# Eighteen feature tiles of a SwiGLU feed-forward by pairs, seven half products in place of eight

## The chip, the cores and the metric

The kernel runs on one core of a Trainium2 chip. The metric is device time in microseconds (us) of the whole kernel, taken over several runs; the trace is that of one execution. Five engines work side by side, each in the order of its own instructions: TensorE (PE, matrix products; PEld is its loading of stationaries), VectorE (DVE), ScalarE (ACT), GpSimd (POOL) and SyncE (SP, which here only issues transfers). Transfers between main memory and the on-chip memory (DMA) run beside them.

## What is computed

One layer of a hybrid decoder on 544 tokens (512 of a prompt, 32 of samples), in fp32. The part that the change touches is the feed-forward behind the second norm:

```python
    h2 = rmsnorm(x, norm2_g)
    x = x + (jax.nn.silu(h2 @ w_ffn_gate) * (h2 @ w_ffn_up)) @ w_ffn_down
```

The model width is 1024, the feed-forward width 2816: 22 feature tiles of 128 columns, each with a product for gate and one for up. Ahead of it lie an input projection, gated linear attention, dilated window attention, a merge and an output projection; behind it the down projection and a last norm.

## The kernel before

Features lie on the 128 partitions, tokens along the free axis, in two halves of 272 (`HA`). A product of 1024 inputs is 8 blocks `k` of 128. To reach fp32 accuracy each operand is split into a high and a low fp32r part (`split`: the high part on ACT, L229, the low part on DVE, L221 or, with a factor, L218), and each product is three: high by high, high by low, low by high. So one feature tile of gate is 8 blocks x 3 x 2 halves = 48 matmuls of 128x128 by 272 columns, all at L215.

Weights come as a stream of tiles in one order. `emit_w` takes the next: SP issues its transfer of 512 KB (`raw`, L260), ACT writes `wh` (and a sum into `mark`), DVE writes `wlo`, POOL copies one number of `mark` (`pace`, L280), which holds POOL back until then, and then issues one transfer of the window caches from memory to memory (L399). `raw`, `wh` and `wlo` have two buffers each, so a tile is prepared while another is multiplied.

In the feed-forward the loop `for m in range(2, NF)` does gate, then up, of one feature tile. `gated` takes the results out: ACT writes tanh into `ts`, DVE makes two operations on `ts` (the second with the product for up), then ACT and DVE split `ts` at once into `ah_m` and `al_m`, the operands of the down projection. That needs 22 blocks, in three weight tiles (`KB`) for each of 8 output tiles. The first two feature tiles are done by halves of the tokens, in between the second norm of the other half (`second`: for each of 8 blocks one operation on DVE, L218, and a split). `gfb`, the gains of the last norm spread over the partitions, is loaded through POOL's queue when a place in memory comes free (L411) and scaled by DVE (L1259), ahead of the first output tile.

The instructions of each engine are put in order by a scheduler ahead of time; an engine never steps past one that waits. Places in the on-chip memory are given by a table of slots at the head of the program.

Of the kernel before, what the change touches and what calls it, by code (L numbers as in the profile page):

```python
# [161 lines left out]
def build(tc, I, O, C):  # L162
# [89 lines left out]
    def emit_w(i, pin=lambda i: i, later=None):  # L252
        ap, k0, nk, c0, m, keep = wl[i]
        raw = wp.tile([P, 8, P], F32, tag="raw", name="raw", bufs=2)
# [906 lines left out]
    n2g = vec_tile("n2g", I["norm2_g"][0], 8)  # L1161
    h2h, h2l = [], []
    for i, (a_, b_) in enumerate(cols):
# [35 lines left out]
        def second(i=i, a_=a_, b_=b_, n=n, tiles=tiles, dgs=dgs):  # L1199
# [12 lines left out]
            if i:  # L1212
                free("acc", "sq", "rt", "r2i", "dg2", "h2")
# [154 lines left out]
```

## Time and profile before

| | |
|---|---|
| three runs | 1081.20, 1082.54 and 1085.53 us, median 1082.54 |
| profiled execution | span 1081.6 us from first to last instruction, no other time on record for it |
| PE busy | 1061.0 us, 98% |
| DVE, ACT, POOL busy | 52%, 38%, 28% |

"Busy" is time with an instruction under way. The profile gives each engine's own queue, what each idle stretch waited for, and the granted clock of TensorE (1.00 is 2.4 GHz, 0.50 is 1.2 GHz). The span lies 0.9 us under the median.

### The profile page before, as it was taken

How to read it: one execution, taken by the hardware profiler on the slowest of the kernel's cores; microseconds unless marked ns; L12 is line 12 of the kernel's file. 1: busy time of each engine (PE TensorE's matmuls, PEld its weight loads, DVE VectorE, ACT ScalarE, POOL GpSimd, SP SyncE). 2: the span in 40 equal slices, each digit the busy share in tenths (PEclk: the TensorE clock that was granted, in tenths of full speed). 3: DMA queues.
4: the chain of work that ended last, by engine and by line, in shares of the span. 5: the costliest groups of instructions: out<-in, count | busy, mean ns of one | idle time of the engine just before them, and what ended most of it. 6: DMA issues, size and time to landing. Idle time of an engine off the chain costs nothing.

```text
span 1081.6 us, 20287 instructions
## 1 busy us (share of the span) xinstructions
PE 1061.0 (98%) x8151; PEld 1025.4 (95%) x8151; DVE 559.7 (52%) x1061; ACT 413.4 (38%) x942; POOL 301.7 (28%) x485
## 2 busy tenths in 40 slices
PE   6999999999999999999999999999999999999997
PEld 5999898999999989989989999999999999999996
DVE  5687764685686645646544565533333333332332
ACT  5454445644464434433333343323232322222232
POOL 2533323233354312222212121122222222322221
PEclk8999999999999999999999999999999999999998
DMA  8588446665677626536424551245454545544442
GB/s 229 142 237 254 142 130 181 185 189 171 188 237 231 219 89 196 156 119 200 137 64 135 183 175 68 90 162 189 164 187 158 192 158 192 188 154 116 113 112 83
DMA packets 178286, 176.14 MB, mean 163 GB/s; under 512 B 9952, under 2 KB 163264, under 8 KB 176912
## 3 DMA queue, kind: packets, MB, share of 16 engines
q1 hardware_dynamic: 155632, 84.36, 28.1%
q0 software_dynamic: 16272, 86.19, 22.7%
q10 hardware_dynamic: 6288, 4.29, 1.3%
q8 instruction: 64, 1.05, 0.4%
q14 instruction: 30, 0.25, 0.1%
HBM read 162.99 MB, written 55.67 MB: 202 GB/s over the span
## 4 chain that ended last, share of the span: by engine, by line
PE 93%; DMA 3%; ACT 1%; DVE 1%; issue 0%; ACTq 0%; POOL 0%; POOLq 0%; DVEq 0%
PE d L215 72%; PE zo L215 5%; PE zB L215 3%; PE zs L215 2%; PE zw L215 2%; PE zl L215 2%; DMA raw<-in_w_in 1%; PE zf L215 1%; PE zu L215 1%; DMA raw<-in_w_out 1%; PE zA L215 1%; DMA x<-in_x_prompt 1%; PE zq L215 1%; PE zA L674 1%; PE zp L215 1%
## 5 line engine op out<-in xcount | busy, mean ns | idle before, releaser
L229 ACT ACTIVATE wh<-raw 128x1024 fp32r<-128x1024 f32 (+1 forms) x133 | 138.5, 1041 | 414.2 <-PE d L215 329.0
L280 POOL COPY pace<-mark 1x1 f32<-1x1 f32 x145 | 123.6, 853 | 590.1 <-ACT wh L229 538.1
L221 DVE TENSOR_TENSOR wlo<-raw,wh 128x1024 fp32r<-128x1024 f32 (+1 forms) x132 | 159.6, 1209 | 203.3 <-ACT wh L229 203.2
L215 PE MATMUL d<-h,wh 128*128 128x272 f32 x1344 | 226.4, 288 | 0.0
L215 PE MATMUL d<-hh,wh 128*128 128x272 f32 (+1 forms) x928 | 203.9, 297 | 3.3 <-ACT hh L229 2.2
L215 PE MATMUL d<-hl,wh 128*128 128x272 f32 (+1 forms) x928 | 201.8, 295 | 0.0
L215 PE MATMUL d<-hh,wlo 128*128 128x272 f32 x912 | 195.4, 293 | 0.0
L215 PEld LDWEIGHTS d<-h,wh 128*128 128x128 f32 x1344 | 191.4, 188 | 0.0
L215 PEld LDWEIGHTS d<-hh,wh 128*128 128x128 f32 (+1 forms) x928 | 148.6, 190 | 6.6 <-ACT hh L229 2.3
L215 PEld LDWEIGHTS d<-hl,wh 128*128 128x128 f32 (+1 forms) x928 | 148.2, 189 | 3.8 <-issue 2.7
L215 PEld LDWEIGHTS d<-hh,wlo 128*128 128x128 f32 x912 | 145.3, 190 | 0.6
L215 PE MATMUL d<-h,wlo 128*128 128x272 f32 x672 | 141.8, 288 | 0.0
L215 PEld LDWEIGHTS d<-h,wlo 128*128 128x128 f32 x672 | 106.6, 188 | 0.0
L215 PE MATMUL d<-ah,wh 128*128 128x272 f32 x308 | 64.2, 290 | 0.0
L215 PE MATMUL d<-ah,wlo 128*128 128x272 f32 x308 | 63.7, 288 | 0.0
L215 PE MATMUL d<-al,wh 128*128 128x272 f32 x308 | 63.5, 287 | 0.0
L221 DVE TENSOR_TENSOR qb<-kt,qb 128x512 f32<-128x512 f32 x48 | 33.0, 688 | 45.0 <-DMA qb<-qd_d 44.8
L215 PEld LDWEIGHTS d<-al,wh 128*128 128x128 f32 x308 | 48.3, 188 | 0.0
L215 PEld LDWEIGHTS d<-ah,wh 128*128 128x128 f32 x308 | 48.3, 188 | 0.1
L215 PEld LDWEIGHTS d<-ah,wlo 128*128 128x128 f32 x308 | 48.2, 188 | 0.0
L221 DVE TENSOR_TENSOR ts<-ts,d 128x544 f32<-128x544 f32 x21 | 15.1, 721 | 62.0 <-PE d L215 62.0
L411 POOL DMA_DIRECT2D kt<-in_state_win_k x48 | 32.9, 685 | 12.2 <-DVE qb L221 9.1
(438 smaller groups left out, 1756.2 us busy)
## 6 DMA issues: line engine op xcount, KB each, us to landing
raw<-in_w_in SPq DMA_DIRECT2D x58, 512.0 KB, 5.8
out_win_k_sample<-in_state_win_k POOLq DMA_DIRECT2D x32, 511.0 KB, 4.6
out_win_v_sample<-in_state_win_v POOLq DMA_DIRECT2D x32, 511.0 KB, 4.7
qb<-qd_d POOLq DMA_DIRECT2D x48, 256.0 KB, 5.1
raw<-in_w_ffn_gate SPq DMA_DIRECT2D x22, 512.0 KB, 5.6
raw<-in_w_ffn_up SPq DMA_DIRECT2D x22, 512.0 KB
kt<-in_state_win_k POOLq DMA_DIRECT2D x32, 256.0 KB, 5.3
vt<-in_state_win_v POOLq DMA_DIRECT2D x32, 256.0 KB, 4.2
```

The source lines that it names most:

```text
L215: return pe.matmul(out, lhsT=lhsT, rhs=rhs, start=start, stop=stop)
L221: return dve.tensor_tensor(out=out, in0=a, in1=b, op=op)
L229: pin(act.activation(out=hi, in_=src, func=AF.Copy, scale=scale, **kw))
L280: tc.keep_in_program_order(pool.tensor_copy(out=pace, in_=mark[0:1]))
L411: tc.keep_in_program_order((eng or nc.gpsimd).dma_start(out=t, in_=ap))
L674: pe.transpose(zA[:, v * P:(v + 1) * P], s[:, v * P:(v + 1) * P], ident)
```

## The change

Feature tiles 0 to 3 stay as they were (`PLAIN = 4`). The other 18 go by pairs, gate and up apart: 9 x 2 = 18 pair products. For one pair, weights (two feature tiles, split into two halves of the 8 blocks) and activations (two halves of the blocks, two halves of the tokens) are taken as 2x2 matrices of parts, and the four results come from seven products of parts, by Strassen's scheme, in place of eight. One such half product has 4 blocks x 3 = 12 matmuls of 272 columns, so a pair has 84.

What that needs:

- Sums of activations, formed once: `n5`, `n6`, `n4`, `n7`, each split in two parts; the normed activations (`hf`) are kept in fp32 until then, and `second` now does all eight operations on DVE ahead of the splits, two blocks at a time.
- Four sums of weights per pair, all on DVE (`sm` twice, `raw` twice, each 128x512), and the splits of five stationaries: `w12` and `w24` (1024 wide), `ws1`, `ws3`, `w22` (512 wide), each with one buffer for its high and one for its low part.
- The results are put together in `t4` by four operations on DVE; ACT copies the results of products 1 and 5 out first (`p1`, `p5`). The products go 1, 5, 2, 6, 7, 3, 4.
- The gated results stay in fp32 (`y_m`) and are split into `ah_m` and `al_m` for the down projection only when slots of the pair products come free, `ah_2` and `al_2` in the slots of `w22`, `gfb` in the slot of `w12h`.
- `raw`, `wh` and `wlo` share six buffers of one tag ("w"), in the whole kernel.

The core of the diff:

```diff
-    wp = opened(base, name="wp", bufs=3)
+    wp = opened(base, name="wp", bufs=6)
...
-        raw = wp.tile([P, 8, P], F32, tag="raw", name="raw", bufs=2)
+        raw = wp.tile([P, 8, P], F32, tag="w", name="raw")
...
-            for m in range(8):
-                t = two.tile([P, HA], F32, tag="h2", name="h2")
-                stt(t[:, 0:n], x2[m][:, a_:b_], n2g[:, m:m + 1], zb[:, 0:n], ALU.mult, ALU.mult)
-                split(h2h[i][m], h2l[i][m], t[:, 0:n])
...
+            for j in range(4):
+                for u in range(2):
+                    m = 2 * j + u
+                    stt(hf[i][j][:, u], x2[m][:, a_:b_], n2g[:, m:m + 1], zb[:, 0:n], ALU.mult, ALU.mult)
+                split(hi[j], lo[j], hf[i][j])
...
+    def prep_12(x):
+        mark = cst.tile([P, 1], F32, name="mark", bufs=8)
+        f = form("w12", raws[x][0], 8, accum_out=mark)
+        sta[x, 1], sta[x, 2] = halves_of(f, 0), halves_of(f, 1)
...
+    def prep_5(x):
+        (r1, r2), sm = raws[x], sms[x]
+        tt(sm[:, 0:4], r2[:, 0:4], r2[:, 4:8], ALU.add)
+        tt(sm[:, 4:8], r2[:, 0:4], r1[:, 0:4], ALU.add)
+        sta[x, 5] = form("ws1", sm[:, 0:4])
...
+    def prep_63(x):
+        r1 = raws[x][0]
+        tt(r1[:, 0:4], sms[x][:, 0:4], r1[:, 0:4], ALU.add)
+        tt(r1[:, 4:8], r1[:, 0:4], r1[:, 4:8], ALU.add)
+        f = form("w24", r1, 8)
+        sta[x, 6], sta[x, 3] = halves_of(f, 0), halves_of(f, 1)
...
+    def prep_7(x):
+        sta[x, 7] = form("ws3", sms[x][:, 4:8])
...
+    def prep_4(x):
+        sta[x, 4] = form("w22", raws[x][1][:, 4:8])
...
+    def product(x, n, z):
+        wh, wlo = sta.pop((x, n))
+        xh, xl = mov[n]
+        for k in range(4):
+            for j, (w, v) in enumerate(((wh, xh), (wh, xl), (wlo, xh))):
+                pin(mm(z, w[:, k], v(k), start=(k == 0 and j == 0), stop=(k == 3 and j == 2)))
...
+        product(x, 6, z[:, 1])
+        tt(t[:, 0:2], z, p1.to_broadcast([P, 2, HA]), ALU.add)
...
+        product(x, 7, z7)
+        tt(t[:, 2], z7, t[:, 1], ALU.add)
+        tt(t[:, 1:4:2], t[:, 1:3], p5.to_broadcast([P, 2, HA]), ALU.add)
...
+        product(x, 4, z[:, 1])
+        tt(t[:, 1:3], z, t[:, 1:3], ALU.add)
...
+    for m in range(NF):
+        ah.append(one.tile([P, NT], F32R, name=f"ah_{m}"))
+        al.append(one.tile([P, NT], F32R, name=f"al_{m}"))
+        split(ah[m], al[m], ym[m], 0.5)
+        free(f"y_{m}")
```

What it moves, at three places. SP's queue at the start of the program, before (a `raw` is a weight tile, an `xT_d` the store of one block of the transposed input):

```order
L260 DMA raw<-in_w_in 128x8x128 x2
L415 DMA xT_d<-xT_109 128x544
L415 DMA xT_d<-xT_110 128x544
L415 DMA xT_d<-xT_111 128x544
L415 DMA xT_d<-xT_112 128x544
L415 DMA xT_d<-xT_113 128x544
L415 DMA xT_d<-xT_114 128x544
L415 DMA xT_d<-xT_115 128x544
L415 DMA xT_d<-xT_116 128x544
L260 DMA raw<-in_w_in 128x8x128 x16
```

And now:

```order
L269 DMA raw<-in_w_in 128x8x128
L424 DMA xT_d<-xT_109 128x544
L424 DMA xT_d<-xT_110 128x544
L424 DMA xT_d<-xT_111 128x544
L424 DMA xT_d<-xT_112 128x544
L424 DMA xT_d<-xT_113 128x544
L424 DMA xT_d<-xT_114 128x544
L424 DMA xT_d<-xT_115 128x544
L424 DMA xT_d<-xT_116 128x544
L269 DMA raw<-in_w_in 128x8x128 x17
```

The second weight tile has moved behind the eight stores.

DVE's queue in the middle of the feed-forward, before: one feature tile is these five rows (numbers behind names tell buffers apart).

```order
L221 TENSOR_TENSOR wlo_9973<-raw_9969,wh_9972 128x1024
L218 SCALAR_TENSOR_TENSOR ts_10030<-ts_10030,d_9979 128x544
L221 TENSOR_TENSOR ts_10030<-ts_10030,d_10043 128x544
L221 TENSOR_TENSOR wlo_10037<-raw_10033,wh_10036 128x1024
L218 SCALAR_TENSOR_TENSOR al_15_10029<-ts_10030,ah_15_10028 128x544
```

And now, from the seventh product of one pair (`t4<-zs`) on: the rows at the turn to the next pair, twelve of fifteen.

```order
L230 TENSOR_TENSOR t4_9157<-zs_9229,t4_9157 128x272
L230 TENSOR_TENSOR raw_9018<-raw_9018 128x512
L230 TENSOR_TENSOR t4_9157<-t4_9157,p5_9186 128x2x272
L230 TENSOR_TENSOR w22l_9281<-raw_9019,w22h_9280 128x512
L230 TENSOR_TENSOR t4_9157<-d_9244,t4_9157 128x544
L230 TENSOR_TENSOR sm_9154<-raw_9153 128x512
L230 TENSOR_TENSOR sm_9154<-raw_9153,raw_9152 128x512
L230 TENSOR_TENSOR w24l_9260<-raw_9018,w24h_9259 128x1024
L227 SCALAR_TENSOR_TENSOR y_8_9284<-y_8_9284,t4_9157 128x544
L227 SCALAR_TENSOR_TENSOR y_9_9287<-y_9_9287,t4_9157 128x544
L230 TENSOR_TENSOR ws1l_9364<-sm_9154,ws1h_9363 128x512
L230 TENSOR_TENSOR w12l_9341<-raw_9152,w12h_9340 128x1024
```

Between the low part of `w22` and that of `w24`, both for the pair that PE takes next, now stand three other operations (`t4`, `sm`, `sm`).

DVE's queue at the turn to the down projection, before: the last split stands alone behind the last result, and `gfb` behind it.

```order
L221 TENSOR_TENSOR ts_10786<-ts_10786,d_10799 128x544
L221 TENSOR_TENSOR wlo_10793<-raw_10789,wh_10792 128x1024
L218 SCALAR_TENSOR_TENSOR al_21_10785<-ts_10786,ah_21_10784 128x544
L221 TENSOR_TENSOR wlo_10866<-raw_10862,wh_10865 128x768
L1259 TENSOR_SCALAR gfb_10851<-gfb_10851 128x1024
L1264 MEMSET ys_10859 128x45
```

And now (`t4_10927` belongs to the last pair; between the last two rows shown and `al_2` stand `al_10`, `al_9`, `al_16`, `al_15`, a `t4` of 544 columns, `al_12`, `al_11`, `al_14` and `al_13`):

```order
L230 TENSOR_TENSOR w24l_10887<-raw_10650,w24h_10886 128x1024
L230 TENSOR_TENSOR wlo_11130<-raw_11126,wh_11129 128x1024
L227 SCALAR_TENSOR_TENSOR al_6_11052<-y_6_9012,ah_6_11051 128x544
L227 SCALAR_TENSOR_TENSOR al_5_11048<-y_5_8743,ah_5_11047 128x544
L230 TENSOR_TENSOR t4_10927<-d_10958,p1_10941 128x544
L227 SCALAR_TENSOR_TENSOR y_20_10911<-y_20_10911,t4_10784 128x544
L227 SCALAR_TENSOR_TENSOR y_21_10914<-y_21_10914,t4_10784 128x544
L1440 TENSOR_SCALAR gfb_11115<-gfb_11115 128x1024
L1445 MEMSET ys_11123 128x45
L227 SCALAR_TENSOR_TENSOR al_19_11104<-y_19_10647,ah_19_11103 128x544
L227 SCALAR_TENSOR_TENSOR al_8_11060<-y_8_9284,ah_8_11059 128x544
L230 TENSOR_TENSOR t4_10927<-zs_10984,t4_10927 128x272
```

Sixteen of the low parts for the down projection have moved to this place, and `gfb` stands in the midst of them.

## Rows read from the trace of the kernel before

**Rows 1.** The page: span, and busy time of the engines.

```profile
span 1081.6 us, 20287 instructions
PE 1061.0 (98%) x8151; PEld 1025.4 (95%) x8151; DVE 559.7 (52%) x1061; ACT 413.4 (38%) x942; POOL 301.7 (28%) x485
```

**Rows 2.** Chain that ended last, pieces around the feed-forward: start us, us, what.

```profile
660.06 3.00 PE zw L215 x24
...
682.77 0.25 PE d L215 x2
...
694.82 264.20 PE d L215 x2100
```

**Rows 3.** Waits, 700 to 930 us: engine, line, releaser, us, times, longest.

```profile
DVE wlo L221 <- ACT wh L229: 86.2, 38, 4.6
DVE ts L221 <- PE d L215: 58.9, 19, 3.1
```

**Rows 4.** Timeline of SP, first and last of eight tiles of gate.

```profile
763.62 0.37 SPq L260 DMA_DIRECT2D raw<-in_w_ffn_gate  x1
...
848.18 0.37 SPq L260 DMA_DIRECT2D raw<-in_w_ffn_gate  x1
```

**Rows 5.** Instructions by form, 700 to 930 us: busy us, mean ns, idle before.

```profile
L221 DVE TENSOR_TENSOR wlo<-raw,wh 128x1024 fp32r<-128x1024 f32 x38 | 46.6, 1225 | 86.2 <-ACT wh L229 86.2
L221 DVE TENSOR_TENSOR ts<-ts,d 128x544 f32<-128x544 f32 x19 | 13.7, 721 | 58.9 <-PE d L215 58.9
```

**Rows 6.** The page, costliest groups: 128x512 on DVE.

```profile
L221 DVE TENSOR_TENSOR qb<-kt,qb 128x512 f32<-128x512 f32 x48 | 33.0, 688 | 45.0 <-DMA qb<-qd_d 44.8
```

**Rows 7.** Timeline of DVE: operations that follow each other without idle time.

```profile
693.48 0.71 DVE L218 SCALAR_TENSOR_TENSOR ts<-ts,d 128x544 f32<-128x544 f32 x1
694.11 1.22 DVE L221 TENSOR_TENSOR wlo<-raw,wh 128x1024 fp32r<-128x1024 f32 x1
695.25 0.71 DVE L221 TENSOR_TENSOR ts<-ts,d 128x544 f32<-128x544 f32 x1
695.88 0.43 DVE L218 SCALAR_TENSOR_TENSOR ts<-ts,zf 128x272 f32<-128x272 f32 x1
```

**Rows 8.** Timeline of DVE: an operation that reads what the one before wrote.

```profile
600.24 0.72 DVE L218 SCALAR_TENSOR_TENSOR ta<-ta,d 128x544 f32<-128x544 f32 x1 [2.71 <-PE d L215]
601.00 0.72 DVE L221 TENSOR_TENSOR ta<-ta,tb 128x544 f32<-128x544 f32 x1
```

**Rows 9.** Timelines of ACT and DVE: a split, and the operation behind it.

```profile
809.50 1.06 ACT L229 ACTIVATE wh<-raw 128x1024 fp32r<-128x1024 f32 x1 [4.42 <-PE d L215]
810.69 1.23 DVE L221 TENSOR_TENSOR wlo<-raw,wh 128x1024 fp32r<-128x1024 f32 x1 [4.26 <-ACT wh L229]
```

**Rows 10.** Timeline of SP at the start, and the page's transfer of a weight tile.

```profile
14.06 4.94 SPq L415 DMA_DIRECT2D xT_d<-xT  x8
raw<-in_w_in SPq DMA_DIRECT2D x58, 512.0 KB, 5.8
```

**Rows 11.** Timeline of DVE in the second norm.

```profile
679.62 0.90 DVE L218 SCALAR_TENSOR_TENSOR h<-xres,n2g,zb 128x272 f32<-128x272 f32 x2
```

**Rows 12.** Timeline where the down projection begins: PE, POOL, DVE.

```profile
936.26 0.42 PE L215 MATMUL d<-ah,wh 128*128 128x272 f32 x2
...
939.13 0.56 POOL L411 DMA_DIRECT2D gfb<-in_norm_f_g  x1
...
945.66 0.69 DVE L1259 TENSOR_SCALAR gfb<-gfb 128x1024 f32<-128x1024 f32 x1 [1.36 <-DMA gfb<-in_norm_f_g]
```

**Rows 13.** Timeline of PE around the start of the first product.

```profile
14.91 2.61 PE L215 MATMUL d<-dgt,ones 128*128 128x128 f32 x10 [1.68 <-DVE dgt L476]
...
19.73 0.82 PE L215 MATMUL d<-hh,wh 128*128 128x272 f32 x2 [2.21 <-ACT hh L229]
...
24.75 0.41 PE L215 MATMUL d<-hl,wh 128*128 128x272 f32 x2
```

**Rows 14.** Windows: span, busy of each engine, granted clock, DMA share, GB/s.

```profile
19.00:24.00 5.00, 4.11 (x15) 3.53 (x16) 4.97 (x7) 3.38 (x6) 0.17 (x1) 0.50 0.59 190
```

More of the change, by code (lines that the diff above doesn't have):

```diff
@@ L264, in emit_w @@
             step = 8
-            wh = [wp.tile([P, 8, P], F32R, tag="wh", name="wh", bufs=2)]
+            wh = [wp.tile([P, 8, P], F32R, tag="w", name="wh")]
             wlo = [wh[0][:, :, 2 * m:3 * m]]
@@ L380, in build @@
         W["wo", m] = want(I["w_out"][0], 0, 8, m * P, keep=f"wo{m}")
-    for m in range(NF):
+    for m in range(PLAIN):
         W["fg", m] = want(I["w_ffn_gate"][0], 0, 8, m * P, keep="fg1" if m == 1 else None)
@@ L1203, in second @@
                 (pin if i else nop)(mm(zb[:, c0:c1], ones[0:w_, :], dgt[0:w_, 0:w_]))
[L1204 to L1210 removed]
+            hi, lo = ([one.tile([P, 2, n], F32R, name=f"h2{i}{w}_{j}") for j in range(4)] for w in "hl")
+            hf.append([one.tile([P, 2, n], F32, name=f"hf{i}_{j}") for j in range(4)])
+            h2h.append([hi[k // 2][:, k % 2] for k in range(KD)])
+            h2l.append([lo[k // 2][:, k % 2] for k in range(KD)])
+            for j in range(4):
[3 more added lines that the diff above has]
+                split(hi[j], lo[j], hf[i][j])
             free(*[f"mg{i}_{m}" for m in range(8)])
             if i:
[L1213 removed]
+                free("acc", "sq", "rt", "r2i", "dg2")
         if i == 0:
@@ L1217, in build @@
             second()
-    ah, al = [], []
     F2, F2L = halved(h2h), halved(h2l)
+    ym = [None] * NF
     def gated(m, zg, zu, parts):
-        ah.append(one.tile([P, NT], F32R, name=f"ah_{m}"))
-        al.append(one.tile([P, NT], F32R, name=f"al_{m}"))
-        ts = two.tile([P, NT], F32, tag="ts", name="ts")
+        t = ym[m] = one.tile([P, NT], F32, name=f"y_{m}")
         for (a_, b_), g_, u_ in zip(parts, zg, zu):
-            t = ts[:, a_:b_]
-            act.activation(out=t, in_=g_, func=AF.Tanh, scale=0.5)
-            stt(t, t, 1.0, g_, ALU.add, ALU.mult)
-            tt(t, t, u_(), ALU.mult)
-            split(ah[m][:, a_:b_], al[m][:, a_:b_], t, 0.5)
+            act.activation(out=t[:, a_:b_], in_=g_, func=AF.Tanh, scale=0.5)
+            stt(t[:, a_:b_], t[:, a_:b_], 1.0, g_, ALU.add, ALU.mult)
+            tt(t[:, a_:b_], t[:, a_:b_], u_(), ALU.mult)
     z4 = {}
-    for hf in range(2):
+    for hf_ in range(2):
         for m in range(2):
@@ L1238, in build @@
                 if m == 0:
-                    z = z4.setdefault((nm, m), dense_ps() if hf == 0 else None)
+                    z = z4.setdefault((nm, m), dense_ps() if hf_ == 0 else None)
                 else:
                     z = z4.setdefault((nm, m), [None, None])
-                    z[hf] = mps("zf")[:, 0:cols[hf][1] - cols[hf][0]]
-                gemm(W[nm, m], F2, F2L, halves=(hf,), z=z, ahead=W["fu", 1] + hf * m - W[nm, m],
-                     fix=hf == 0, mid=(AT[m, nm], rates if m == 0 else second) if hf == 0 and (m, nm) in AT else None)
-            if hf == 1:
+                    z[hf_] = mps("zf")[:, 0:cols[hf_][1] - cols[hf_][0]]
+                gemm(W[nm, m], F2, F2L, halves=(hf_,), z=z, ahead=W["fu", 1] + hf_ * m - W[nm, m],
+                     fix=hf_ == 0, mid=(AT[m, nm], rates if m == 0 else second) if hf_ == 0 and (m, nm) in AT else None)
+            if hf_ == 1:
                 if m == 0:
@@ L1251, in build, with parts_of, operand @@
     dropped("fu1")
-    for m in range(2, NF):
-        zg = gemm(W["fg", m], F2, F2L)
-        gated(m, [zg], [lambda: gemm(W["fu", m], F2, F2L)], [(0, NT)])
-    free("ts", *[f"h2{i}_{m}" for i in range(2) for m in range(8)])
+    def parts_of(h, l):
+        return [lambda k, t=t: t[k // 2][:, k % 2] for t in (h, l)]
+    def operand(nm, src):
+        hi, lo = ([one.tile([P, 2, HA], F32R, name=f"{nm}{w}_{j}") for j in range(2)] for w in "hl")
+        for j in range(2):
+            split(hi[j], lo[j], src[j])
+        return parts_of(hi, lo)
@@ new lines, in by_halves, with summed_up @@
+    def by_halves(i, k0):
+        return [lambda k, t=t: t[i][k0 + k] for t in (h2h, h2l)]
+    B11, B12, B21, B22 = hf[0][0:2], hf[1][0:2], hf[0][2:4], hf[1][2:4]
+    mov = {1: by_halves(0, 0), 2: by_halves(0, 4), 3: by_halves(1, 4)}
+    def summed_up(nm, f):
+        ts_ = [two.tile([P, 2, HA], F32, tag="nf", name=nm, bufs=4) for _ in range(2)]
+        for j in range(2):
+            f(j, ts_[j])
+        return ts_
+    n5 = summed_up("n5", lambda j, t: tt(t, B11[j], B12[j], ALU.subtract))
@@ new lines, in build @@
+    mov[5] = operand("n5", n5)
+    n6 = summed_up("n6", lambda j, t: stt(t, n5[j], -1.0, B22[j], ALU.mult, ALU.subtract))
+    mov[6] = operand("n6", n6)
+    n4 = summed_up("n4", lambda j, t: stt(t, n6[j], -1.0, B21[j], ALU.mult, ALU.subtract))
+    mov[4] = operand("n4", n4)
+    n7 = summed_up("n7", lambda j, t: tt(t, B22[j], B12[j], ALU.subtract))
+    mov[7] = operand("n7", n7)
+    free("nf", *[f"hf{i}_{j}" for i in range(2) for j in range(4)])
+    pairs = [(nm, m) for m in range(PLAIN, NF, 2) for nm in ("fg", "fu")]
@@ new lines, in build, with fetch, form @@
+    src_of = {"fg": I["w_ffn_gate"][0], "fu": I["w_ffn_up"][0]}
+    raws, sms, sta = {}, {}, {}
+    def fetch(x):
+        nm, m = pairs[x]
+        r1, r2, sm = (wp.tile([P, 8, P], F32, tag="w", name=n) for n in ("raw", "raw", "sm"))
+        raws[x], sms[x] = (r1, r2), sm
+        c1, c2 = (src_of[nm][:, c * P:(c + 1) * P].rearrange("(k p) n -> p k n", p=P) for c in (m, m + 1))
+        nc.sync.dma_start(out=r1, in_=c1)
+        nc.sync.dma_start(out=r2, in_=c2)
+    def form(nm, src, n=4, **kw):
+        hi, lo = (two.tile([P, n, P], F32R, tag=f"{nm}{w}", name=f"{nm}{w}", bufs=1) for w in "hl")
+        split(hi, lo, src, **kw)
+        return hi, lo
@@ new lines, in halves_of @@
+    def halves_of(f, i):
+        return [t[:, 4 * i:4 * i + 4] for t in f]
+    def prep_12(x):
+        mark = cst.tile([P, 1], F32, name="mark", bufs=8)
+        f = form("w12", raws[x][0], 8, accum_out=mark)
+        sta[x, 1], sta[x, 2] = halves_of(f, 0), halves_of(f, 1)
+        pace = cst.tile([1, 1], F32, name="pace", bufs=2)
+        pin(pool.tensor_copy(out=pace, in_=mark[0:1]))
+        for _ in range(2):
+            if side_dma:
+                side_dma.pop(0)()
+    def prep_5(x):
[3 more added lines that the diff above has]
+        sta[x, 5] = form("ws1", sm[:, 0:4])
@@ new lines, in copied, with use @@
+    def copied(z, nm):
+        t = two.tile([P, 1, HA], F32, tag=nm, name=nm, bufs=1)
+        act.copy(out=t[:, 0], in_=z)
+        return t
+    def use(x, t):
+        nm, m = pairs[x]
+        for i in range(2):
+            g = t[:, 2 * i:2 * i + 2].rearrange("p a n -> p (a n)")
+            if nm == "fg":
+                y = ym[m + i] = one.tile([P, NT], F32, name=f"y_{m + i}")
+                act.activation(out=y, in_=g, func=AF.Tanh, scale=-0.5 if i else 0.5)
+                stt(y, y, 1.0, g, ALU.add, ALU.mult)
+            else:
+                tt(ym[m + i], ym[m + i], g, ALU.mult)
@@ new lines, in single, with double, pair @@
+    def single():
+        return mps("zs")[:, 0:HA]
+    def double():
+        z = psd.tile([P, 1024], F32, tag="d", name="d").rearrange("p (b n) -> p b n", n=512)
+        return z[:, :, 0:HA]
+    def pair(x):
+        nxt = x + 1 < len(pairs)
+        if x + 2 < len(pairs):
+            fetch(x + 2)
+        t = two.tile([P, 4, HA], F32, tag="t4", name="t4")
+        z1 = single()
+        product(x, 1, z1)
+        p1 = copied(z1, "p1")
+        z5 = single()
+        product(x, 5, z5)
+        p5 = copied(z5, "p5")
+        z = double()
+        product(x, 2, z[:, 0])
+        if nxt:
+            prep_12(x + 1)
+        product(x, 6, z[:, 1])
+        tt(t[:, 0:2], z, p1.to_broadcast([P, 2, HA]), ALU.add)
+        if nxt:
+            prep_5(x + 1)
+        z7 = single()
+        product(x, 7, z7)
+        tt(t[:, 2], z7, t[:, 1], ALU.add)
+        tt(t[:, 1:4:2], t[:, 1:3], p5.to_broadcast([P, 2, HA]), ALU.add)
+        z = double()
+        product(x, 3, z[:, 0])
+        if nxt:
+            prep_63(x + 1)
+            prep_7(x + 1)
+        product(x, 4, z[:, 1])
+        tt(t[:, 1:3], z, t[:, 1:3], ALU.add)
+        if nxt:
+            prep_4(x + 1)
+        use(x, t)
@@ new lines, in build @@
+    for m in range(2, PLAIN):
+        zg = gemm(W["fg", m], F2, F2L, ahead=min(2, W["fu", PLAIN - 1] - W["fg", m]))
+        if m == PLAIN - 1:
+            fetch(0)
+            fetch(1)
+            for f in (prep_12, prep_5, prep_63, prep_7, prep_4):
+                f(0)
+        gated(m, [zg], [lambda: gemm(W["fu", m], F2, F2L, ahead=min(2, W["fu", PLAIN - 1] - W["fu", m]))], [(0, NT)])
+    free(*[f"h21{w}_{j}" for w in "hl" for j in range(2)])
+    last_x = len(pairs) - 1
+    for x in range(len(pairs)):
+        if x == last_x:
+            weights(W["fd", 0, 0], 0)
+        pair(x)
@@ new lines, in build @@
+    free("p1", "p5", "t4", *[f"{n}{w}" for n in ("w12", "w24", "ws1", "ws3", "w22") for w in "hl"])
+    free(*[f"h20{w}_{j}" for w in "hl" for j in range(2)])
+    free(*[f"n5{w}_{j}" for w in "hl" for j in range(2)])
+    free(*[f"h20{w}_{j}" for w in "hl" for j in range(2, 4)])
+    free(*[f"n6{w}_{j}" for w in "hl" for j in range(2)])
+    free(*[f"h21{w}_{j}" for w in "hl" for j in range(2, 4)])
+    free(*[f"n{n}{w}_{j}" for n in (4, 7) for w in "hl" for j in range(2)])
+    ah, al = [], []
```

10 lines of the change are left out of this document (4 added, 6 removed), and 96 rows, old and new, of the table PLACE.

## Prediction

> **What bounds the kernel now.** The page first: PE is busy for 1061.0 of 1081.6 us, DVE for 52% [rows 1]. Then the chain that ended last: from 694.82 us it is one piece of 264.20 us, 2100 products without a break, so the feed-forward runs at the pace of PE alone [rows 2]. The waits of that stretch say the same from the other side: PE is not among the waiting, DVE waits 38 times for a high part and 19 times for a result [rows 3]. So every product removed there is time gained, as long as DVE, which gets the new work, stays ahead. The pace: SP issues a gate tile at 763.62 and the eighth at 848.18 us, 84.56 us for seven feature tiles of 96 products, 12.08 each, 125.8 ns per product [rows 4].
>
> **What is removed.** 18 pair products of 84 in place of 96: 216 products, 216 x 0.1258 = -27.2 us. A half product uses a stationary once, where the feed-forward used most of them for both halves of the tokens. The output projection does that already: `zw`, 24 such products in 3.00 us, 125 ns each [rows 2]. So no price for it.
>
> **DVE's load.** A pair needs on DVE two operations of 1024, seven of 512, five of 544 and one of 272. By duration: 1225 and 721 ns [rows 5], 688 for 512 [rows 6], 0.43 us for 272 [rows 7], in sum 2 x 1.225 + 7 x 0.688 + 5 x 0.72 + 0.43 = 11.30 us. That is more than the 84 x 0.1258 = 10.57 us of PE. But operations that follow each other start before the one ahead has ended: 544 to the next 0.63 us, 1024 to the next 1.14 [rows 7], both some 0.085 less than the duration. With 0.60 and 0.35 for the other two kinds, worked out by the same 0.085, a pair takes 2.28 + 4.20 + 3.15 + 0.35 = 9.98, about 10.0 us. DVE is then busy for 95% of a pair: it just keeps up, and what counts is its order at the turn.
>
> The Trainium skill, VectorE: DVE Perf Modes, section "The DRAIN you can't avoid", says that a next operation does not start until the pipe of the one ahead is empty, and that a semaphore costs nothing more. [Rows 7] speak against the strict reading, an operation that reads the result of the one ahead [rows 8] for it. Its case is the second rival below.
>
> **The turn of a pair, in the steady part.** Let E be the end of a pair's last product. All of `w22` has one buffer, which that product holds. ACT writes the high part of 512 by about E+0.74, DVE its low part from 0.13 us later (as from 809.50 + 1.06 to 810.69, [rows 9]), E+0.87. Then `t4` (from E+1.47), `sm`, `sm`, and `w24l` from E+3.3 to E+4.57. PE does products 1, 5 and 2 first, 36 x 0.1258 = 4.53, and asks for the low part of `w24` after two more, at E+4.78. The margin is 0.2 us in the best case. Over the eleven pairs from the fourth on I take 0.1 us each, +1.1 (0 to 6: 0.55 us at each, if two hand-overs of that 0.13 and the full durations of two operations come in). Pair 0 comes in while the plain tiles' work is still on DVE, with `ws1l` and `w24l` late by 0.4 and 0.7: +1.1 (0.5 to 2). In the pair before the last, `ws1l` for the last waits for a buffer that product 5 holds, in front of `t4` and `w24l`: +1.6 (1 to 2.5).
>
> **The start.** The second weight tile went out with the first; now it stands behind the eight stores, which SP issues from 14.06 to 19.00 us [rows 10]. With 3.8 to 5.8 us of transfer it is there at 23 to 25, its high part about 1.1 later. PE starts at 19.73 at half clock, 0.41 us for two [rows 13] become 0.82, and has twelve products before it needs it, till about 22.9. +1.5 (0 if PE is late anyway, 3).
>
> **The weights in the middle.** One pool of six buffers lets a transfer wait for what PE frees. A tile is needed each 12 us, a transfer takes 5.8 [rows 10]: 0, with 2 either way.
>
> **The second norm.** Before, DVE made two operations (0.90 us) and then low parts [rows 11]. Now all eight (3.6 us from 679.62) and a sum stand ahead of the first low part, which is ready at about 684.3; PE asks for it near 683.1, 0.25 after the first products of the second half [rows 2]. +1.3 (0.8 to 1.8). The sums of activations then lie beside the two plain tiles that are left.
>
> **The turn to the down projection.** Before, it came without a gap, `al_21` alone being new, and `gfb` was waited for by DVE only, which had time [rows 12]. Now the order puts sixteen low parts and `gfb` between the last `w24l` and `al_2`, and PE takes blocks 0, 1, 2 in this order. With E the end of the pair before the last: `w24l` ends at E+4.6, then one of 1024, two of 544, `t4`, two `y`: E+8.9. `gfb` lies in `w12h`'s slot, free after product 2 of the last pair (E+4.5); from issue to DVE's start took 945.66 - 939.13 = 6.5 us [rows 12], so DVE waits till E+11.2. Then `gfb` 0.65, a memset of 0.1, twelve of 544 (7.6), one of 272 (0.35), and `al_2` itself 0.72: E+20.6. PE has 10.57 for the last pair and fourteen products, 1.76: it asks at E+12.3. Stall +8.2 (5.5 without the wait for `gfb`, 10 by durations). What comes later (`al_18`, `al_20`, `al_21`) has 16 blocks of PE's time.
>
> **The clock.** A PE that stands 8 us does not come back at full speed. At the start, after its pause up to 19.73, its clock is 0.50 through 19 to 24 us [rows 14] and two products take 0.82 us; at 24.75 they take 0.41 [rows 13]. Those 4.6 us at half pace cost half of it, +2.3 (0 if the clock stays, 3).
>
> **Sum.** -27.2 + 1.5 + 0 + 1.3 + 1.1 + 1.1 + 1.6 + 8.2 + 2.3 = -10.1. The span of 1081.6 becomes 1071.5; as the median of the runs lies 0.9 above that span, **1072.4 us**. The terms' ends make 1063 to 1080 likely if this is the case.
>
> **Rivals.**
> *The turn to the down projection is cheaper.* If `gfb` is not waited for (a transfer that starts or lands 2.3 us earlier) and the clock stays, 4.6 us less: 1067.8. For it: a PE with little to do in front may be slow to lose its clock. Against it: [rows 13]. Chance 0.15.
> *DVE is the bound of all pairs.* If the operations don't overlap, because most of them wait for something, a pair takes 11.30, 0.73 more than PE's, x 17 = 12.4 in place of the 3.8 of the three turn terms: 1081.0. For it: fifteen operations, most with a wait for ACT, PE or each other; DVE before was half idle [rows 3], so no row shows it under full load. By the page of the Trainium skill named above this is what happens, and [rows 7] are against it. Chance 0.15.
> *Slower: each operation on DVE is held until the one ahead is quite done.* A dependent operation starts 0.76 us after one of 0.72 [rows 8], 0.04 behind its end. If each of the fifteen did, a pair takes 11.30 + 0.60 = 11.9, 1.33 over PE's, x 17 = 22.6 in place of 3.8: 1091.2. The gain is gone from 10.57 + (10.1 + 3.8)/17 = 11.39 us per pair on, and it is slower by 0.5% from 11.7. For it: chains such as `sm`, `raw`, `w24h`, `w24l`. Against it: the scheduler puts other work between most of them. Chance 0.07.
>
> **How the numbers follow.** The forecast case has 0.63. From no change a measurement here tells some 0.5%, 5.4 us: 1077.1 to 1088. Faster: 0.15, and 0.55 of the forecast case, 0.70. Same: the 0.08 that is left of it and 0.12 of the second rival, 0.20. Slower: the third rival and the rest, 0.10. The range from 1063 to 1084 holds the forecast case and the first two rivals and leaves out the third.
>
> **What would show it.** Behind: products of a pair in about 10.6 us, and issues of `raw` for successive pairs as far apart; if 11.3, the second rival, if 11.9, the third, and DVE busy without idle time. PE waits: for `al` at one place, some 8 us, and behind it a stretch with the clock at 0.50; for `wh` near 23 us, 1.5; for `h21l` near 683, 1.3; for `w24l` in each pair, 0.1. DVE's wait for `gfb`: about 2.3. The forecast is wrong if the wait for `w24l` or `ws1l` is over 0.5 us at every pair, or that at the turn to the down projection under 4.

## The result, and the profile after

The changed kernel takes 1091.45 us (median of four runs, 1089.47 to 1092.65) against 1083.12 before: a ratio of 1.0077, 95% interval 1.0058 to 1.0096. It is slower, where 1072.4 was forecast, and the time lies above the range. It is nearly the time of the third rival (1091.2), but not by its mechanism, as the profile shows.

The page of the changed kernel, headline, busy time and the chain that ended last:

```profile
span 1090.7 us, 20137 instructions
PE 1044.2 (96%) x7935; PEld 1004.4 (92%) x7935; DVE 680.9 (62%) x1266; ACT 460.6 (42%) x1013; POOL 263.5 (24%) x467
...
PE 77%; DMA 12%; DVE 4%; ACT 3%; issue 2%; POOL 1%; ACTq 0%; POOLq 0%; SPq 0%; DVEq 0%
```

Against [rows 1] there are 216 products fewer, as there should be, and PE is 16.8 us less busy. But the chain, which was PE's at 93% before, now holds 12% of transfers, where it held 3%. The same line of the kernel before:

```profile
PE 93%; DMA 3%; ACT 1%; DVE 1%; issue 0%; ACTq 0%; POOL 0%; POOLq 0%; DVEq 0%
```

To see where, the program is cut at an instruction that both kernels have: the small products `zc` of the second norm's second half, just ahead of the feed-forward. In the chain of the kernel before, and in that of the changed one:

```profile
672.48 0.47 PE zc L215 x6
```

```profile
694.85 0.47 PE zc L224 x6
```

Ahead of this point the changed kernel loses 22.4 us. Behind it, it takes 1090.7 - 694.85 = 395.9 us where the kernel before took 409.1: a gain of 13.3. The windows tell the same, before and after (span, then busy time and instructions of PE, PEld, DVE, ACT and POOL, then the granted clock, the DMA share and GB/s):

```profile
100.00:660.00 560.00, 559.00 (x4224) 528.28 (x4223) 339.75 (x724) 246.42 (x552) 160.25 (x266) 0.99 0.53 164
```

```profile
100.00:660.00 560.00, 543.34 (x4060) 510.62 (x4059) 332.09 (x706) 242.65 (x541) 145.45 (x266) 0.99 0.54 164
...
800.00:840.00 40.00, 40.00 (x322) 40.00 (x321) 38.35 (x58) 18.89 (x34) 9.61 (x12) 1.00 0.64 199
930.00:960.00 30.00, 23.52 (x162) 22.99 (x161) 19.70 (x30) 13.45 (x26) 3.41 (x6) 0.83 0.31 101
```

Between 100 and 660 us, where the diff changes only the buffers of the weight stream and one place in the table of slots, PE is idle for 16.7 us where it was for 1.0, and does 164 products fewer. In the pairs (800 to 840) it has no idle time at all, with DVE busy for 96%. At the turn to the down projection (930 to 960) it stands for 6.5 us, and the granted clock of these 30 us is 0.83 in the mean.

PE's waits in the changed kernel from 680 to 960 us, where all the new work lies (engine, line, releaser, us in total, times, longest):

```profile
PE d L224 <- ACT ah L238: 3.5, 1, 3.5
PE d L224 <- DVE al L227: 3.0, 1, 3.0
PE d L224 <- DVE w24l L230: 1.3, 2, 1.0
PE zs L224 <- DVE ws1l L230: 1.2, 1, 1.2
PE d L224 <- DVE h21l L230: 1.0, 1, 1.0
```

In the kernel before PE has no wait there. The waits stand at the places that the prediction named, with two differences: at the turn to the down projection 3.5 us are a wait for ACT's `ah_2`, where only DVE's `al_2` was named, and no pair in the middle waits for `w24l`. And SP's timeline of the pairs, first and last of eight issues:

```profile
801.35 0.37 SPq L1305 DMA_DIRECT2D raw<-in_w_ffn_gate  x1
...
874.90 0.37 SPq L1305 DMA_DIRECT2D raw<-in_w_ffn_up  x1
```

Seven pairs in 73.55 us, 10.51 each, 125.1 ns per product.

So the loss lies ahead of the feed-forward. PE's waits from 100 to 660 us, the longest of three before, and the three longest of sixteen rows after:

```profile
PE d L215 <- ACT mg L229: 0.5, 1, 0.5
```

```profile
PE zo L224 <- ACT wh L238: 3.1, 1, 3.1
PE zt L952 <- ACT vn L933: 1.8, 1, 1.8
PE zt L692 <- ACT ob L688: 1.6, 1, 1.6
```

The engines that handle the weights wait for something else than before. SP's waits to issue a tile and ACT's at `wh`, before and after:

```profile
SPq L260 <- DVE wlo L221: 649.3, 108, 18.6
...
ACT wh L229 <- PE d L215: 329.0, 91, 5.9
...
ACT wh L229 <- DMA raw<-in_w_in: 5.5, 1, 5.5
```

```profile
SPq L269 <- PE d L224: 565.4, 72, 22.6
...
ACT wh L238 <- DMA raw<-in_w_in: 123.1, 42, 7.6
```

SP waited for DVE's split of an earlier tile; now it waits for products on PE. ACT stood at `wh` before too, 91 times, but for a buffer that PE was still using; for a tile of `w_in` to land it waited once. Now it does 42 times. One such place, in timelines of SP, ACT and PE of the changed kernel:

```profile
364.62 0.38 SPq L269 DMA_DIRECT2D raw<-in_w_in  x1
...
370.13 0.57 ACT L933 COPY vn<-zv 128x512 f32<-128x512 f32 x1
374.55 1.06 ACT L238 ACTIVATE wh<-raw 128x1024 fp32r<-128x1024 f32 x1 [3.84 <-DMA raw<-in_w_in]
...
375.60 0.57 ACT L933 COPY vn<-zv 128x512 f32<-128x512 f32 x1
...
376.22 0.32 PE L952 MATMUL zt<-ident,v 128*96 128x128 f32 x1 [1.75 <-ACT vn L933]
```

SP issues at 364.62, and the chain has a group of PE's products ending 0.05 us ahead of it. The tile lands 9.82 us later, as the chain shows:

```profile
364.62 9.82 DMA raw<-in_w_in
```

ACT has come to `wh` at 370.7 and stands for 3.84 us; behind it in its order stands the copy `vn`, which has nothing to do with weights, and PE waits for that. Followed back through the trace in this way, eight of PE's 17 waits of over 0.2 us between 100 and 660 us, 7.5 of the 16.7 us, begin with a tile of `w_in` that ACT stood for, and one of 1.5 us with a tile of `w_out`. Four, 4.8 us with the longest of all, begin with the transfer of a window cache, and four with no transfer. The same copy and split in the kernel before:

```profile
359.67 0.59 ACT L924 COPY vn<-zv 128x512 f32<-128x512 f32 x1
361.29 1.06 ACT L229 ACTIVATE wh<-raw 128x1024 fp32r<-128x1024 f32 x1 [1.02 <-POOL qm L1046]
```

No wait for a transfer: its tile had landed. But the order has changed too: there both copies `vn` stood ahead of this split, the second at 359.67 and the split at 361.29, and its tile could not have held them up.

### The profile page after: what moved, and what is told of

It reads as the page before. It is cut to its first block, busy times and chain, and to the rows that moved or that the text cites. A ratio compares the mean times of both kernels' runs of the same rounds, so it can differ in the third digit from the quotient of the medians.

```text
span 1090.7 us, 20137 instructions
## 1 busy us (share of the span) xinstructions
PE 1044.2 (96%) x7935; PEld 1004.4 (92%) x7935; DVE 680.9 (62%) x1266; ACT 460.6 (42%) x1013; POOL 263.5 (24%) x467
## 4 chain that ended last, share of the span: by engine, by line
PE 77%; DMA 12%; DVE 4%; ACT 3%; issue 2%; POOL 1%; ACTq 0%; POOLq 0%; SPq 0%; DVEq 0%
PE d L224 52%; PE zs L224 9%; DMA raw<-in_w_in 6%; PE zo L224 4%; PE zB L224 2%; DMA vt<-in_state_win_v 2%; PE zw L224 2%; PE zl L224 2%; DMA raw<-in_w_out 1%; DMA x<-in_x_prompt 1%; PE zu L224 1%; ACT wh L238 1%; DVE al L227 1%; PE zf L224 1%; PE zA L224 1%
## 5 line engine op out<-in xcount | busy, mean ns | idle before, releaser
L230 DVE TENSOR_TENSOR wlo<-raw,wh 128x1024 fp32r<-128x1024 f32 (+1 forms) x96 | 115.8, 1207 | 147.1 <-ACT wh L238 81.5
L238 ACT ACTIVATE wh<-raw 128x1024 fp32r<-128x1024 f32 (+1 forms) x97 | 100.4, 1035 | 238.7 <-DMA raw<-in_w_in 123.1
L224 PE MATMUL d<-hh,wlo 128*128 128x272 f32 x912 | 199.0, 295 | 0.3 <-DVE wlo L230 0.3
L289 POOL COPY pace<-mark 1x1 f32<-1x1 f32 x109 | 58.9, 540 | 442.4 <-ACT wh L238 389.9
L1321 POOL COPY pace<-mark 1x1 f32<-1x1 f32 x18 | 25.6, 1424 | 144.2 <-ACT w12h L238 144.2
L230 DVE TENSOR_TENSOR vl<-vt,vh 128x512 fp32r<-128x512 f32 (+1 forms) x40 | 24.9, 634 | 31.1 <-ACT vh L238 30.9
L238 ACT ACTIVATE vh<-vt 128x512 fp32r<-128x512 f32 (+1 forms) x40 | 22.8, 585 | 31.2 <-DMA vt<-in_state_win_v 19.4
L552 DVE TENSOR_REDUCE sall<-qb 128x8 f32<-128x512 f32 x48 | 32.7, 682 | 0.8
L420 POOL DMA_DIRECT2D vt<-in_state_win_v x40 | 21.8, 547 | 43.8 <-DVE vl L230 38.1
```

The source lines that it names most:

```text
L224: return pe.matmul(out, lhsT=lhsT, rhs=rhs, start=start, stop=stop)
L230: return dve.tensor_tensor(out=out, in0=a, in1=b, op=op)
L238: pin(act.activation(out=hi, in_=src, func=AF.Copy, scale=scale, **kw))
L289: tc.keep_in_program_order(pool.tensor_copy(out=pace, in_=mark[0:1]))
L420: tc.keep_in_program_order((eng or nc.gpsimd).dma_start(out=t, in_=ap))
L552: dve.tensor_reduce(out=sall[:, g, 16 * b_:16 * b_ + 16].rearrange("p (t h) -> p t h", h=4)[:, :, 2 * hp:2 * hp + 2], in_=qb.rearrange("p ...
```

## The experiments

The theory (A): in the shared pool a transfer is issued only when PE has freed a buffer, too late for ACT, and that is the loss ahead of the feed-forward. The rival (B): it comes from elsewhere, such as other places of small tiles. Times in the first column of rows are of each kernel's own trace; "behind `zc`" is the span from the cut above to the end.

**Own buffers in the changed kernel** (e1_own_buffers). The pairs take their three tiles from the same six buffers:

```diff
-        raw = wp.tile([P, 8, P], F32, tag="w", name="raw")
+        raw = wp.tile([P, 8, P], F32, tag="raw", name="raw", bufs=2)
...
-            wh = [wp.tile([P, 8, P], F32R, tag="w", name="wh")]
-            wlo = [wp.tile([P, 8, P], F32R, tag="w", name="wlo")]
+            wh = [wp.tile([P, 8, P], F32R, tag="wh", name="wh", bufs=2)]
+            wlo = [wp.tile([P, 8, P], F32R, tag="wlo", name="wlo", bufs=2)]
...
-        r1, r2, sm = (wp.tile([P, 8, P], F32, tag="w", name=n) for n in ("raw", "raw", "sm"))
+        r1, r2, sm = (wp.tile([P, 8, P], F32, tag=g, name=n, bufs=2) for n, g in (("raw", "raw"), ("raw", "wh"), ("sm", "wlo")))
```

> The changed kernel, with the weight stream on two buffers each for raw, wh and wlo as before; the pairs take their three tiles from the same six buffers. Theory A (in the shared pool a transfer is issued only when PE frees a buffer, and the 22 us lost ahead of the feed-forward are that): they come back, 1091.4 becomes 1069 to 1073, no wait of PE behind a weight transfer between 60 and 660 us, and the feed-forward begins near 676 as before. Theory B (they come from elsewhere, such as the other places of small tiles or more traffic): still 1088 to 1094.

Measured: 1074.28 us, ratio to before 0.9922 (0.9901 to 0.9943). `zc` stands at 671.03 us, so the 22.4 us are back to the last of them. The time is a little above the expectation. Behind `zc` it takes 400.9 us, 5.0 more than the changed kernel, and in the trace the pairs begin worse: PE does 31 products in place of 82 in one stretch of 10 us.

```profile
720.00:730.00 10.00, 6.81 (x31) 6.47 (x31) 8.48 (x13) 5.13 (x8) 0.00 (x0) 0.66 0.41 118
```

There pair 0 waits for its second weight tile, which takes `wh`'s buffer and so again one that PE frees. SP's waits for the second tiles from 690 to 735 us:

```profile
SPq L1306 <- PE d L224: 8.9, 2, 5.8
```

**The pool alone, in the kernel before** (e2_pool_alone). `raw`, `wh` and `wlo` of the kernel before with tag "w" and six buffers, nothing else.

> The kernel before, with nothing but the shared pool of six buffers for raw, wh and wlo. Theory A: the whole loss without any pair, 1083 becomes 1100 to 1108 (some 20 us ahead of the feed-forward, and perhaps a little in it, where a tile is needed each 6 us). Theory B: 1081 to 1086.

Measured: 1102.93 us, ratio 1.0192 (1.0153 to 1.0230), without any pair. `zc` stands at 689.83, 17.4 us later than before, and behind it the kernel takes 409.2 us, as before. SP's and ACT's waits have turned as in the changed kernel:

```profile
SPq L260 <- PE d L215: 763.9, 111, 22.0
...
ACT wh L229 <- DMA raw<-in_w_in: 114.0, 41, 8.8
ACT wh L229 <- DMA raw<-in_w_ffn_up: 88.0, 20, 6.2
```

Theory A holds as far as the pool is the cause. In the feed-forward ACT waits for transfers too, and that costs nothing; that nothing urgent stands behind `wh` in ACT's order there is the likely reason, and was not tested.

**Only `raw` on its own** (e3_raw_own). The kernel before, `raw` with two buffers of its own, `wh` and `wlo` from one pool of four:

```diff
-            wh = [wp.tile([P, 8, P], F32R, tag="wh", name="wh", bufs=2)]
-            wlo = [wp.tile([P, 8, P], F32R, tag="wlo", name="wlo", bufs=2)]
+            wh = [wp.tile([P, 8, P], F32R, tag="w", name="wh", bufs=4)]
+            wlo = [wp.tile([P, 8, P], F32R, tag="w", name="wlo", bufs=4)]
```

> The kernel before, with raw on its own two buffers and one shared pool of four for wh and wlo. Theory A in the narrow form (what counts is that raw's buffer was freed by DVE's split and is now freed by PE's products): 1081 to 1086, no change. Rival (any sharing that leaves the buffer to the order worked out ahead of time costs): 1088 or more.

Measured: 1082.81 us, ratio 0.9995 (0.9980 to 1.0011): no change. SP waits for DVE again:

```profile
SPq L260 <- DVE wlo L221: 651.3, 108, 18.7
```

So sharing among the operands costs nothing; what costs is that `raw` shares their buffers, which the products free. Two things come with that, and no run parts them: the tile comes later, and the order of the instructions, which is worked out ahead of time, is another. Compared product by product up to `zc`, 4955 of PE's 4962 products keep their order in e3_raw_own, 3356 in e2_pool_alone and 3329 in the changed kernel. A run with the shared pool in the old order would tell, and was not made.

**The slots at the exit** (e4_slots_at_exit). The changed kernel, shared pool and all, with the table's places for the down projection's operands handed on by one or more, so that the first operands get the places that come free first. Of 30 entries:

```diff
-    "ah_2": (40,), "al_2": (54,), "ah_3": (10,), "al_3": (6,), "ah_4": (93,), "al_4": (3,)
+    "ah_2": (10,), "al_2": (6,), "ah_3": (93,), "al_3": (3,), "ah_4": (17,), "al_4": (41,)
...
-    "ah_16": (66,), "al_16": (37,)
+    "ah_16": (40,), "al_16": (54,)
```

> The changed kernel, with the slots of the down projection's operands handed out in the order in which they come free, so that ah_2 and al_2 lie in those of product 1 and ah_16 and al_16 in those of w22. Theory (the stall there is al_2 behind a chain on DVE): the 6.5 us of PE's waits and the 2 to 2.5 us of half clock behind them go, 1091.4 becomes 1081 to 1084. Rival (DVE is simply behind with sixteen splits, and another of them is late in its place): 1086 to 1091, with PE waiting for another al.

Measured: 1085.08 us, its ten runs between 1075.26 and 1090.90; ratio to before 1.0007 (0.9978 to 1.0035). Median against median it lies 6.4 us under the changed kernel, between the two expectations. The trace decides: behind `zc` it takes 385.9 us against 395.9, 10.0 less, and the exit is full, at full clock:

```profile
930.00:960.00 30.00, 30.00 (x240) 29.88 (x239) 24.82 (x37) 17.65 (x33) 4.52 (x8) 1.00 0.49 149
```

The part ahead of the feed-forward was 5.0 us longer in this trace (`zc` at 699.83), with the same shared pool and the same order of PE's products. Its row from 100 to 660 us:

```profile
100.00:660.00 560.00, 543.19 (x4025) 510.07 (x4024) 330.48 (x701) 242.55 (x539) 144.05 (x265) 0.98 0.54 162
```

PE is as long idle as in the changed kernel (543.19 us busy against 543.34), so what differs there is the clock. In windows of 20 us the granted clock is below 1.00 four times (0.83, 0.91, 0.83, 0.83), in the changed kernel three times (0.91, 0.92, 0.82). That is some 24 us at half clock against 14, an estimate from these windows, and half of the difference, 5.0 us, is lost. Why the clock falls more often in one execution than in another was not settled.

**Both** (e5_both). e1_own_buffers with the slots of e4_slots_at_exit, and a pair's two weight tiles both in `raw`'s or both in `wlo`'s buffers:

```diff
-        r1, r2, sm = (wp.tile([P, 8, P], F32, tag="w", name=n) for n in ("raw", "raw", "sm"))
+        r1, r2, sm = (wp.tile([P, 8, P], F32, tag=g, name=n, bufs=2) for n, g in (("raw", ("raw", "wlo")[x % 2]), ("raw", ("raw", "wlo")[x % 2]), ("sm", "wh")))
```

> The changed kernel with both: own buffers for raw, wh and wlo (a pair's two weight tiles now both in raw's or both in wlo's buffers in turn, its sums in wh's, so that pair 0 gets its second tile early) and the slots at the exit in the order in which they come free. Theory: with own buffers alone PE did 31 products in place of 82 in the 10 us where the pairs begin (6.4 us lost, of which some 2 stay) and 164 in place of some 246 in the 30 us of the exit (10 us lost, of which 1 stays); 1074.3 becomes 1060 to 1063. Rival (what is taken away comes back as another wait, since DVE is full through all pairs): 1066 to 1074.

Measured: 1062.96 us, ratio to before 0.9811 (0.9796 to 0.9826), faster than both kernels. `zc` stands at 670.46, and 390.4 us are left. That is 4.6 more than in e4_slots_at_exit. The order of DVE's work has changed with the buffers, and PE now waits a little at seven pairs:

```profile
PE d L224 <- DVE w24l L230: 5.2, 7, 2.0
```

**DVE loaded more** (e6_two_more_sums). The first sum of each pair made three times.

```diff
+        tt(sm[:, 0:4], r2[:, 0:4], r2[:, 4:8], ALU.add)
+        tt(sm[:, 0:4], r2[:, 0:4], r2[:, 4:8], ALU.add)
         tt(sm[:, 0:4], r2[:, 0:4], r2[:, 4:8], ALU.add)
```

> The kernel of e5_both, with the first sum of weights made three times over, so two more operations of 128x512 on DVE per pair, results unchanged. If operations on DVE follow each other as in the trace of before (0.60 us each, 10.0 per pair) a pair takes some 11.2 us and PE becomes the one that waits: 0.7 us at each of 17 pairs, 12 us more than e5_both, 1072 to 1076. If the chip held each until the one ahead was quite done, 11.30 us and then 12.7, e5_both itself would already be slow, and this would be 24 us slower. If DVE had room to spare: no change.

Measured: 1077.23 us, 14.3 above e5_both; 402.2 us behind `zc`, 11.7 more. SP's timeline, first and last of nine issues:

```profile
787.32 0.37 SPq L1305 DMA_DIRECT2D raw<-in_w_ffn_up  x1
...
877.25 0.37 SPq L1305 DMA_DIRECT2D raw<-in_w_ffn_up  x1
```

Eight pairs in 89.93 us, 11.24 each: ten from the fifteen operations, 1.2 from two more, by the intervals of [rows 7]. DVE has no idle time left, and PE waits at every pair:

```profile
PE d L224 <- DVE w24l L230: 11.7, 18, 2.5
```

**Sums on GpSimd** (e7_sums_on_pool). Two of a pair's four sums moved from DVE to POOL.

```diff
-        tt(sm[:, 0:4], r2[:, 0:4], r2[:, 4:8], ALU.add)
-        tt(sm[:, 4:8], r2[:, 0:4], r1[:, 0:4], ALU.add)
+        pool.tensor_tensor(out=sm[:, 0:4], in0=r2[:, 0:4], in1=r2[:, 4:8], op=ALU.add)
+        pool.tensor_tensor(out=sm[:, 4:8], in0=r2[:, 0:4], in1=r1[:, 0:4], op=ALU.add)
```

> The kernel of e5_both, with the first two sums of weights of each pair on GpSimd in place of VectorE, so two operations of 128x512 fewer there. Theory (DVE is nearly full but PE sets the pace in the steady part): within 2 us of e5_both. Rival (the remaining waits of PE in the pairs are DVE's load): 2 to 5 us faster.

Measured: 1071.34 us, 8.4 slower than e5_both, with 5.6 more behind `zc` in the traces (396.0 against 390.4); theory and rival were both wrong. DVE has less to do and takes longer. Its timeline, and POOL's over the same stretch:

```profile
807.63 3.55 DVE L230 TENSOR_TENSOR raw<-sm,raw 128x512 f32<-128x512 f32 x1
811.10 0.43 DVE L230 TENSOR_TENSOR t<-zs,t 128x272 f32<-128x272 f32 x1
...
808.08 1.30 POOL L1328 TENSOR_TENSOR sm<-raw 128x512 f32<-128x512 f32 x1
809.33 1.28 POOL L1329 TENSOR_TENSOR sm<-raw 128x512 f32<-128x512 f32 x1
```

An addition of 0.68 us takes 3.55 while POOL makes two. From 740 to 920 us this addition takes 1.14 us in the mean, where it took 0.69 in e5_both; one that reads a result of PE (`t<-d,p`) takes 0.71 in one and 0.72 in the other.

**Product 7 ahead of product 6** (e8_product7_first). e5_both with the order 1, 5, 2, 7, 6, 3, 4:

```diff
+        z7 = single()
+        product(x, 7, z7)
         product(x, 6, z[:, 1])
         tt(t[:, 0:2], z, p1.to_broadcast([P, 2, HA]), ALU.add)
...
-        z7 = single()
-        product(x, 7, z7)
```

> The kernel of e5_both with product 7 ahead of product 6, so that PE asks for the low part of w24 twelve products (1.5 us) later, the rest as it is. Theory (what is left at the turn of a pair is one late low part, 5.2 us over seven pairs, the longest 2.0): nearly all of it goes, 1063.0 becomes 1058 to 1060, and PE waits for w24l for less than 1 us in all. Rival (DVE is full, so the wait moves to another stationary, ws3 or w22): 1061 to 1064.

Measured: 1063.82 us, no gain; the rival was right that the wait moves, though not in where to. Behind `zc` it takes 390.0 us against 390.4. The wait for `w24l` shrinks and another takes its place, for the result buffer that `t` frees:

```profile
PE d L224 <- DVE t L230: 3.6, 3, 2.3
...
PE d L224 <- DVE w24l L230: 1.8, 3, 0.9
```

## Why the prediction was wrong

**The step that failed is "The weights in the middle"**: 0, with 2 either way, because a tile was said to be needed each 12 us and a transfer to take 5.8. Measured: the loss ahead of `zc` is 22.4 us in the changed kernel and 17.4 with the pool alone. Three things were wrong or left out. First, the 12 us are a misreading: [rows 4] list the tiles of gate alone, and one of up lies between each two. SP's timeline before:

```profile
703.22 0.37 SPq L260 DMA_DIRECT2D raw<-in_w_ffn_gate  x1
709.17 0.37 SPq L260 DMA_DIRECT2D raw<-in_w_ffn_up  x1
```

That is a tile each 6 us in the feed-forward. Between 100 and 660 us SP issues 66 whole tiles before, one each 8.5 us in the mean, so the room over a transfer was some 3 us and not 6. A single transfer took 9.82 us in this stage, above the median of [rows 10], but one of 9.79 stands in the chain of the kernel before too (at 174.52), so the transfers had not become slower. Second, the prediction said of moved transfers what they wait for, but not what waits behind them: ACT takes `wh` in its order, and the attention's copies and splits stand behind it, so a tile that lands 4 us late for ACT makes PE wait for a thing that is no weight. Third, it reckoned with no other order of the instructions in this stage. Part of the room is gone when the transfer is issued at the end of PE's products and not at the end of DVE's split, and the order itself changed; how much is due to each stays open.

PE's idle time between 100 and 660 us rose from 1.0 to 16.7 us, 15.7 of the 22.4. The granted clock of that stretch adds an estimated 3.5 (windows of 20 us put 14 us at half clock against 7 before) and the start 0.7; some 2.5 us are not accounted for. At the place shown above the stretch from 380 to 388 us has a granted clock of 0.56:

```profile
380.00:388.00 8.00, 8.00 (x43) 8.00 (x42) 4.76 (x13) 3.56 (x7) 0.69 (x2) 0.56 0.29 96
```

The signs of being wrong that the prediction named (over 0.5 us at every pair, or under 4 at the turn to the down projection) did not come, because none of them looked ahead of the feed-forward.

**The products removed**: right. 216 fewer, at 125.1 ns 27.0 us.

**The start**: +1.5 forecast; a group of 96 products in the first weights' stretch ends 0.7 us later than before (55.55 against 54.87).

**The second norm**: +1.3 forecast, and PE waits 1.0 for `h21l`.

**The turn of a pair**: +3.8 forecast in three terms. Pair 0 waits 1.2 for `ws1l` and 0.3 for `w24l`, the pair before the last 1.0, the eleven in the middle not at all. The margin of 0.2 us in the sum held at each, with DVE idle for 0.41 us in most pairs, where `w22l` waits for its high part. That fits the 10.0 us of DVE's work against 10.5 of PE's.

**DVE's rate, the second and the third rival**: refuted, though the time of the third came true. A pair takes 10.51 us, not 11.3 or 11.9. The Trainium skill, VectorE: DVE Perf Modes, section "The DRAIN you can't avoid", lets the next operation start only when the pipe is empty; by that alone, as an estimate from the durations of [rows 5] to [rows 7], a pair would take the 11.30 us of the second rival. The same section adds that a next operation which is not held starts earlier, and the prediction's strict reading left that out. The rows agree with the addition: operations of 0.68 us follow at 0.60 under full load too, and e6_two_more_sums, where DVE has no idle time and sets the pace, gives 11.24 per pair for seventeen operations.

**The turn to the down projection**: +8.2 and +2.3 forecast. PE stands for 3.5 us ahead of `ah_2` and 3.0 ahead of `al_2`. In the 10 us from 935 to 945 it is busy for 3.5 us, at a mean clock of 0.75, and from 945 to 950, at 0.50, it does 24 products where it does 40 at full clock. In e4_slots_at_exit both waits are gone, and with them 10.0 us; the 3.5 us that are not waits are, as far as the windows show, the clock. The wait for `gfb` that the sum counted in did not come: DVE reached it at 934.83, with 5.4 us gone since the issue at 929.40, and did not stand. By the prediction's own figures the stall is then 8.2 - 2.3 = 5.9 us (it says 5.5); 6.5 were measured.

Together the terms behind `zc` were forecast at -11.6 us, from -27.2 + 1.3 + 3.8 + 8.2 + 2.3, and measured at -13.3: 27.0 us of products, less 1.0, 2.5 and 10.0, make 13.5. With its own buffers again (e1_own_buffers) the kernel takes 1074.28 us, 1.9 above the forecast, but that nearness is in part luck: behind `zc` it gains 8.2 us where 11.6 were forecast. The only term of the sum that was wrong by more than 2 us lies ahead of `zc`, in a stage that the change was not about.

## What to carry to other kernels

Let buffers that a transfer lands in be freed by the engine that empties them, not by the one that uses what was made of it: in this kernel sharing `raw`'s buffers with the products' operands cost 1.9% on its own, and sharing the operands' among themselves nothing. A row that lists one kind of tile does not give the time between tiles of all kinds. A prediction of a late transfer has to name what stands behind the instruction that waits for it, on that engine, in each stage of the program. And when a tile table is written anew, hand places that come free early to what is asked for early: that alone took 10 us from the part behind `zc`.

## What the runs showed of the hardware

Here moving work from DVE to POOL was worse than keeping it. In e7_sums_on_pool a POOL addition of two fp32 operands in on-chip memory took 1.3 us at the least and 1.6 to 1.8 in the mean, and a DVE addition that overlapped two of them took 3.55 us in place of 0.68. The Trainium skill, SBUF — State Buffer, section "SBUF: two separate sides", says that the two engines hold one pair of ports in turn, each for a whole instruction, when DVE reads two operands from that memory and GpSimd reads it too. The rows agree that one engine stands for the other's whole instruction: the addition of 3.55 us ends at 811.18, 0.57 us behind the second of POOL's, and of a pair's operations on DVE all but the three that read a result of PE are of that kind. That section of the Trainium skill gives the ports to the one that starts first, and that the rows do not show: the DVE addition is on record 0.45 us ahead of POOL's, and yet it is the one that stands (the profile's times of POOL are rough).

DVE starts an operation some 0.08 us before the one ahead of it ends, for as long as it is loaded, also one such as `w22l`, which needs a high part of ACT, when that was ready in time. The exception is an operation that reads what the one ahead wrote: it starts 0.76 us after one of 0.72 [rows 8]. In e6_two_more_sums DVE is busy for 40.00 of 40 us, and three of its operations there start 0.60 us apart:

```profile
800.00:840.00 40.00, 38.17 (x298) 37.29 (x298) 40.00 (x60) 18.58 (x32) 8.30 (x12) 1.00 0.66 206
...
819.69 0.68 DVE L230 TENSOR_TENSOR sm<-raw 128x512 f32<-128x512 f32 x1
820.29 0.68 DVE L230 TENSOR_TENSOR w22l<-raw,w22h 128x512 fp32r<-128x512 f32 x1
820.89 0.72 DVE L230 TENSOR_TENSOR t<-t,p 128x544 f32<-128x544 f32 x1
```
